# A two-layer HGRN2/mLSTM transformer with experts: router logits from unnormalised rows, expert groups carried across experts, and one order made from simulated times

## The chip, the cores and the metric

The kernel runs on one core of one Trainium2 chip. Its metric is the device time of one execution in microseconds, as a median of runs. The core's engines each work through their own instruction list in order: PE (matmuls and transposes), DVE and ACT (element-wise work), POOL (a few small operations and indirect transfers), and SP, which here issues nearly all DMA transfers.

## The reference, cut to what matters

Two layers on 512 rows of x (and 256 context rows), 1024 wide, all in float32:

```python
for l in range(DEPTH):                         # DEPTH = 2
    mod_x = silu(c) @ w_ada[l] + b_ada[l]      # six vectors of 1024
    hx = x * (1 + mod_x[1]) + mod_x[0]
    mix_x, mix_c = _token_mix(hx, hc, ...)     # w_in, HGRN2 and mLSTM scans, w_out
    x = _layer_norm(ALPHA * x + mod_x[2] * mix_x, ln_g[l, 0], ln_b[l, 0])
    hx = x * (1 + mod_x[4]) + mod_x[3]
    f_x = _channel_mix(hx, l, ...)             # layer 0: dense SwiGLU, layer 1: experts
    x = _layer_norm(ALPHA * x + mod_x[5] * f_x, ln_g[l, 1], ln_b[l, 1])

def _moe_swiglu(h, router_w, router_b, w_gate_up, w_down):      # layer 1
    top_val, top_idx = lax.top_k(h @ router_w + router_b, 2)    # 8 experts
    top_p = softmax(top_val)
    # sum over experts e of combine[:, e] * _swiglu(h, w_gate_up[e], w_down[e])
```

The context rows go through the same steps in layer 0 and end with the mixing of layer 1.

## The kernel before

Every large product is made of three matmuls on operands split into a high and a low part (`wh`, `wl` and `xh`, `xl`, `mm3`, lines 165 to 167), so that weights come by DMA into `wr`, ACT makes `wh` (lines 134, 149) and DVE `wl` (lines 135, 150), 128x1024 elements at a time. In product blocks with 64 rows the two parts of the rows share one matmul, and line 1408 adds the two halves.

The program starts with the conditioning product (`w_ada`, line 275), loads the x and context rows (`xs`, line 932), transposes, scales and splits them, and runs `w_in`. Then come, in layer 0, the two scans, `w_out` and the dense block, and in layer 1 the same scans, `w_out` and the experts.

**Router.** In the last pass of layer 1 over `w_out` each row tile (128 rows; there are four) gets its product (line 979), the residual (`add_x`, line 961), its statistics, and is normalised in place (`finish`, line 893) and stored in `xhd`. `router_tile` then transposes the normalised tile in eight blocks (line 1107), copies them into `xhatT`, and forms the logits (line 1114) with a router matrix `rws` into which scale factors of the conditioning are folded. `router` adds the bias (line 1603) and finds the two best experts; in `moe` ranks are counted by a matmul with ones (lines 1136, 1137), row indices are formed by matmuls with one-hots (line 1213), rows are gathered from `xhd` (line 1245) and transposed (line 1256; `xf` and `xs` are the scaled and split result, lines 1259 to 1263). Beside this, lines 1145 to 1154 scale `xhatT`, transpose it back and store it as residual rows `xd` for the end.

**Experts.** The eight experts are sorted by load into ranks with fixed capacities (256, 192, 128 or 64 rows), in two streams, (0, 1, 2) and (6, 3, 7, 4, 5), whose steps a small planner interleaves by the costs they yield. One expert runs over groups of 256 hidden columns. `first` makes gate and up for a group and `hs` = silu(gate) * up; `turn` transposes `hs` into `hT` (line 1421; lines 1422 and 1423 copy and split it); `second` multiplies by the down weights into accumulators kept for the whole expert. A 256-row expert makes `hT` directly. The order in the code is:

```python
            for f0, nb in groups:
                hT, s = yield from first(f0, nb)
                if prev:
                    yield from second(*prev)
                    yield rates[-1] * prev[2]
                turn(hT, s, nb)
                prev = hT, f0, nb
```

A negative cost in a yield asks the planner to take the same stream next. In the last expert of a stream `ahead` loads what the end needs. After the experts, each row tile gathers its two expert results, adds the residual and is normalised (lines 1565 to 1580).

The instruction lists are made by the framework's scheduler, which orders what the code emits by its own priorities and dependencies; pools of buffers (three `hs`, for instance) limit it.

## Time and profile before

| | |
|---|---|
| time, median of 3 runs (lowest to highest) | 2205.84 us (2203.29 to 2208.99) |
| profiled execution: its time, its span | 2203.97 us, 2201.9 us |
| mean granted clock of PE | 0.968 of full speed |
| busy: PE, PEld, DVE, ACT, POOL | 2065.7, 1748.0, 1463.9, 888.5, 162.4 us |
| DMA | 331.25 MB, mean 150 GB/s |

The span is the stretch that the profiler recorded, from the first instruction to the last. Busy times are sums over each engine's instructions; PE is matmuls, PEld the weight loads beside them. [...] In a timeline or a list of waits, the name behind `<-` in brackets is what ended an engine's idle time. A line number is that of the kernel before.

### The profile page before, as it was taken

The page shows a single profiled execution, that of the slowest core. Times are in us where ns is not written, and L with a number is a line of the kernel's source. Part 1 is how long each engine was busy: PE and PEld are TensorE (multiplying, and loading weights), DVE is VectorE, ACT ScalarE, POOL GpSimd, SP SyncE. Part 2 cuts the span into 40 slices and gives each one's busy share as a digit, 9 for nine tenths or more (in the row PEclk, how much of TensorE's full clock was granted, in tenths as well). Part 3 has the DMA queues.
Part 4 walks back from the last instruction along what each step waited for, and adds up shares of the span by engine and source line. Part 5 has one row for each costly group of instructions (what it writes and reads, how often), then busy time and mean ns, then how long its engine had stood idle before and what let it go on. Part 6 is the DMA issues. An engine that isn't in the chain of part 4 may idle for free. (4 is left out here: it accounts for less than half of the span.)

```text
span 2201.9 us, 31832 instructions
## 1 busy us (share of the span) xinstructions
PE 2065.7 (94%) x12321; PEld 1748.0 (79%) x12321; DVE 1463.9 (66%) x2524; ACT 888.5 (40%) x1409; POOL 162.4 (7%) x163
## 2 busy tenths in 40 slices
PE   8999799999999999999999999999979899798993
PEld 3887688987888888888888788899977787577882
DVE  4466784825787755554555678686678767877776
ACT  3335333323442222211124354334157665766662
POOL 1001000100200000022000000101310000000002
PEclk9999999999999999999999999999869899899996
DMA  7123202146454443322131321124368778888884
GB/s 259 50 69 110 63 27 85 46 142 225 165 183 149 155 138 134 134 77 77 58 106 50 91 68 55 48 63 151 133 210 301 260 265 279 266 271 295 306 280 171
DMA packets 233187, 331.25 MB, mean 150 GB/s; under 512 B 13904, under 2 KB 181012, under 8 KB 233032
## 3 DMA queue, kind: packets, MB, share of 16 engines
q1 hardware_dynamic: 229624, 318.09, 43.5%
q0 software_dynamic: 3408, 11.08, 1.5%
q8 instruction: 99, 1.62, 0.3%
q14 instruction: 56, 0.46, 0.1%
HBM read 304.94 MB, written 24.19 MB: 149 GB/s over the span
## 5 line engine op out<-in xcount | busy, mean ns | idle before, releaser
L165 PE MATMUL g<-xh,wh 128*128 128x512 f32 (+1 forms) x1168 | 400.7, 343 | 1.4 <-ACT xh L380 1.4
L166 PE MATMUL g<-xl,wh 128*128 128x512 f32 (+1 forms) x1168 | 400.3, 343 | 1.5 <-DVE xl L381 1.5
L167 PE MATMUL g<-xh,wl 128*128 128x512 f32 (+1 forms) x1168 | 399.8, 343 | 0.0
L135 DVE TENSOR_TENSOR wl<-wr,wh 128x1024 fp32r<-128x1024 f32 x240 | 293.5, 1233 | 144.0 <-ACT wh L134 142.6
L134 ACT ACTIVATE wh<-wr 128x1024 fp32r<-128x1024 f32 x240 | 249.8, 1056 | 248.7 <-PE sc L167 81.6
L165 PE MATMUL g<-wh,xh 128*128 128x256 f32 x1024 | 296.6, 290 | 9.4 <-ACT wh L134 2.2
L166 PE MATMUL g<-wl,xh 128*128 128x256 f32 x1024 | 296.4, 290 | 2.9 <-DVE wl L131 2.7
L167 PE MATMUL g<-wh,xl 128*128 128x256 f32 x1024 | 294.0, 288 | 0.0
L165 PEld LDWEIGHTS g<-xh,wh 128*128 128x128 f32 x1168 | 220.4, 189 | 30.0 <-issue 1.7
L166 PEld LDWEIGHTS g<-xl,wh 128*128 128x128 f32 x1168 | 220.2, 189 | 27.9 <-DVE xl L381 1.9
L167 PEld LDWEIGHTS g<-xh,wl 128*128 128x128 f32 x1168 | 220.2, 189 | 26.5
L150 DVE TENSOR_TENSOR wl<-wr,wh 128x1024 fp32r<-128x1024 f32 x154 | 185.7, 1219 | 47.6 <-ACT wh L149 46.3
L165 PEld LDWEIGHTS g<-wh,xh 128*128 128x128 f32 x1024 | 196.5, 192 | 15.3 <-ACT slot L766 2.9
L166 PEld LDWEIGHTS g<-wl,xh 128*128 128x128 f32 x1024 | 196.7, 192 | 5.0 <-DVE wl L131 4.4
L167 PEld LDWEIGHTS g<-wh,xl 128*128 128x128 f32 x1024 | 196.4, 192 | 0.0
L149 ACT ACTIVATE wh<-wr 128x1024 fp32r<-128x1024 f32 x154 | 160.4, 1055 | 60.5 <-DMA wr<-in_moe_w_gate_up 43.6
L865 DVE TENSOR_TENSOR s<-g,s 128x512 f32<-128x512 f32 (+1 forms) x44 | 24.4, 555 | 128.4 <-PE g L167 128.4
L463 PE MATMUL sc<-tmp,s 128*128 128x128 f32 x560 | 79.8, 290 | 4.6 <-DVE tmp L471 3.9
L866 ACT ACTIVATE hh<-s 128x512 fp32r<-128x512 f32 (+1 forms) x44 | 23.1, 525 | 144.8 <-DVE s L865 144.8
L463 PEld LDWEIGHTS sc<-tmp,s 128*128 128x128 f32 x560 | 71.6, 193 | 11.2 <-issue 3.9
L520 POOL TENSOR_TENSOR ss<-ss,mhalf 128x4 f32<-128x4 f32 (+1 forms) x22 | 27.3, 1248 | 716.1 <-DVE ss L519 543.5
L458 ACT ACTIVATE s<-slot 128x768 f32<-128x768 f32 (+1 forms) x56 | 44.4, 793 | 78.7 <-DVE slot L469 67.0
(497 smaller groups left out, 4031.9 us busy)
## 6 DMA issues: line engine op xcount, KB each, us to landing
wr<-in_moe_w_gate_up SPq DMA_DIRECT2D x176, 512.0 KB
wr<-in_moe_w_down SPq DMA_DIRECT2D x88, 512.0 KB
wr<-in_w_in SPq DMA_DIRECT2D x64, 512.0 KB
wr<-in_ffn_w_gate_up SPq DMA_DIRECT2D x44, 512.0 KB
wh<-in_w_ada SPq DMA_DIRECT2D x20, 1024.0 KB
wl<-in_w_ada SPq DMA_DIRECT2D x20, 1024.0 KB
wr<-in_ffn_w_down SPq DMA_DIRECT2D x22, 512.0 KB
wr<-in_w_ada SPq DMA_DIRECT2D x16, 512.0 KB
```

The costliest lines, as they stand in the source:

```text
L134: nc.scalar.activation(fl(h), r, AF.Copy)
L135: nc.vector.tensor_tensor(fl(lo), r, fl(h).bitcast(F32), OP.subtract)
L149: nc.scalar.activation(v(h, u), r, AF.Copy)
L150: nc.vector.tensor_tensor(v(lo, u), r, v(h, u).bitcast(F32), OP.subtract)
L165: nc.tensor.matmul(out, ah, bh, start=(i == 0), stop=False)
L166: nc.tensor.matmul(out, ah, bl, start=False, stop=False)
L167: nc.tensor.matmul(out, al, bh, start=False, stop=(i == n - 1))
L458: nc.scalar.activation(apx(kc, 0, [[2 * hh, qn // (2 * hh)], [hh, 2], [1, hh]]), apx(ka, 0, [[2 * hh, qn // (2 * hh)], [hh + T, 2], [1, hh ...
L463: nc.tensor.matmul(pl[:, c - a], kc[:, c * P:(c + 1) * P], apx(qa, c * P + T, [[2 * hh, 64 // hh], [hh - T, 2], [1, hh]]), start=True, sto ...
L520: nc.gpsimd.tensor_tensor(ss[:, :n], ss[:, :n], self.mhalf[:, :n], OP.pow)
L865: nc.vector.tensor_tensor(s, pu, s, OP.mult)
L866: nc.scalar.activation(hh[:, b, t0:t0 + n], s, AF.Copy)
```

## The change

The change has four parts.

1. `TileContext` is opened with `schedule_with_timeline_sim=True`: the scheduler orders all instructions of the program on all engines by a simulated timeline of engines and queues.
2. Router: `router_half` transposes each half of a row tile as soon as the residual is added, before it is normalised, and forms raw logits. In `router`, eight small instructions add minus the mean times the column sums of `rws` (`rsum`, made once by eight matmuls with ones), scale by the reciprocal deviation and add the bias. The normalised rows `xo` go to `xhd` as before.
3. Residual rows are no longer made by transposing `xhatT` back and stored in `xd`; `ahead` loads the rows from `xhd` and two broadcast rows, and eight 1024-wide DVE instructions (`scale`, `shift`) are handed out over the steps of the last big expert.
4. Experts: a group's `turn` and `second` are carried into the next group (`run`), also from one expert into the next of its stream; `turn` is called by `mid` in the middle of the next gate/up product. `rest` finishes the last one. The accumulators are taken when the first `second` begins. `hs` has four buffers. Some small tiles of the planning code share storage (not shown).

```diff
@@ -984,17 +984,20 @@
                     add_x(t, 1)
-                    self.finish(pre[:, t], sts[t], (self.xhd if last else self.xd)[t * P:(t + 1) * P])
+                    if last:
+                        self.router_half(pre, t, 0)
+                        self.router_half(pre, t, 1)
+                        self.router_finish(pre[:, t], sts[t], t, self.xhd[t * P:(t + 1) * P])
+                        continue
+                    self.finish(pre[:, t], sts[t], self.xd[t * P:(t + 1) * P])
                     for u in behind(t, nt):
-                        if last:
-                            self.router_tile(pre, u)
-                        else:
-                            self.split_tile(pre[:, u], u, xh, xl, aff[u // NX], act=u < nt - 2)
+                        self.split_tile(pre[:, u], u, xh, xl, aff[u // NX], act=u < nt - 2)
...
-                self.moe(l, aff[0], pre)
+                self.moe(l, aff[0])
                 break
@@ -1086,34 +1089,44 @@
             nc.sync.dma_start(self.ysd[NSLOT + b * P:NSLOT + (b + 1) * P], zt)
-        self.xt = lp.tile([P, KT, TX], F32, name="xhatT")
+        self.mr = lp.tile([P, NX, 2], F32, name="meanr")
...
-        pb = self.psum("sc", [P, N_E])
-        for k in range(KT):
-            nc.tensor.matmul(pb, self.ones, rt[:, k], start=k == 0, stop=k == KT - 1)
-        nc.vector.tensor_tensor(self.rb, self.rb, pb, OP.add)
+        pb = self.psum("sc", [P, 2, N_E])
+        for i, w in enumerate((rt, self.rws)):
+            for k in range(KT):
+                nc.tensor.matmul(pb[:, i], self.ones, w[:, k], start=k == 0, stop=k == KT - 1)
+        nc.vector.tensor_tensor(self.rb, self.rb, pb[:, 0], OP.add)
+        self.rsum = lp.tile([P, N_E], F32, name="rsum")
+        nc.vector.tensor_copy(self.rsum, pb[:, 1])
         self.plog = self.psum("tr", [P, NX, N_E])
-    def router_tile(self, pre, t):
-        nc = self.nc
-        for hf in range(2):
-            pt = self.psum(("sc", "o")[hf], [P, 4, P])
-            for k in range(4):
-                nc.tensor.transpose(pt[:, k], pre[:, t, (4 * hf + k) * P:(4 * hf + k + 1) * P], self.ident)
-            o = self.xt[:, 4 * hf:4 * hf + 4, t * P:(t + 1) * P]
-            if hf:
-                nc.vector.tensor_copy(o, pt)
-            else:
-                nc.scalar.activation(o, pt, AF.Copy)
-        for k in range(KT):
-            nc.tensor.matmul(self.plog[:, t], self.xt[:, k, t * P:(t + 1) * P], self.rws[:, k], start=(k == 0), stop=(k == KT - 1))
-    def moe(self, l, aff, pre):
+    def router_half(self, pre, t, hf):
+        nc = self.nc
+        pt = self.psum(("sc", "o")[hf], [P, 4, P])
+        for k in range(4):
+            nc.tensor.transpose(pt[:, k], pre[:, t, (4 * hf + k) * P:(4 * hf + k + 1) * P], self.ident)
+        o = self.lp.tile([P, 4, P], F32, tag="preT", name=self.nm("preT"), bufs=4)
+        nc.scalar.activation(o, pt, AF.Copy)
+        for k in range(4):
+            nc.tensor.matmul(self.plog[:, t], o[:, k], self.rws[:, 4 * hf + k], start=hf == 0 and k == 0, stop=hf == 1 and k == 3)
+    def router_finish(self, x, st, t, dst):
+        nc = self.nc
+        mean, r = self.moments(st)
+        nc.vector.tensor_scalar(self.mr[:, t, 0:1], mean, -1.0, None, op0=OP.mult)
+        nc.vector.tensor_copy(self.mr[:, t, 1:2], r)
+        o = self.lp.tile([P, D], F32, tag="xo", name=self.nm("xo"), bufs=2)
+        nc.vector.tensor_scalar(o, x, mean, r, op0=OP.subtract, op1=OP.mult)
+        nc.sync.dma_start(dst, o)
+    def moe(self, l, aff):
@@ -1134,26 +1147,8 @@
         nc.tensor.matmul(pp, self.ones, Mc, start=True, stop=False)
-        mm = nc.tensor.matmul(pp[:, 0:NX], self.trif, M, start=False, stop=True)
-        p0 = tc.cur_priority
-        tc.cur_priority = p0 + 1000
-        gb = self.lp.tile([P, 2, KT], F32, name="gbcol")
-        for i, v in enumerate((self.g_col(l, 0), self.b_col(l, 0))):
-            nc.vector.tensor_scalar(gb[:, i], v, ALPHA, None, op0=OP.mult)
-        for k in range(KT):
-            nc.scalar.activation(self.xt[:, k], self.xt[:, k], AF.Identity, scale=gb[:, 0, k:k + 1], bias=gb[:, 1, k:k + 1])
-        with tc.issue_after(mm.ins):
-            for hf in range(2):
-                for t in range(NX):
-                    pt = self.psum("g", [P, 4, P])
-                    for k in range(4):
-                        nc.tensor.transpose(pt[:, k], self.xt[:, 4 * hf + k, t * P:(t + 1) * P], self.ident)
-                    nc.scalar.activation(pre[:, t, hf * 512:hf * 512 + 512], pt.rearrange("p k c -> p (k c)"), AF.Copy)
-                    if hf:
-                        nc.sync.dma_start(self.xd[t * P:(t + 1) * P], pre[:, t])
+        nc.tensor.matmul(pp[:, 0:NX], self.trif, M, start=False, stop=True)
         self.lp_cm.__exit__(None, None, None)
-        tc.cur_priority = p0
         inc, cnt = small([NX, 8], "inc"), small([8], "cnt")
@@ -1350,23 +1345,22 @@
         def act(pg, pu, shape, parts=P):
-            s = mp.tile([P, 256], F32, tag="hs", name=self.nm("hs"), bufs=3)[:parts, :shape]
+            s = mp.tile([P, 256], F32, tag="hs", name=self.nm("hs"), bufs=HSB)[:parts, :shape]
...
         def expert(n, xs, gu_src, dn_src, acc_tag, write, weight):
...
-            acc = [[self.psum(acc_tag, [P, 512]) for _ in range(2)] for _ in range(nblk)]
-            groups = [(f0, min(256, D_E - f0) // P) for f0 in range(0, D_E, 256)]
-            def first(f0, nb):
+            acc = []
+            def first(f0, nb, mid):
                 fn = nb * P
@@ -1383,6 +1377,8 @@
                         yield 4
+                        if b == 0:
+                            mid()
                     return hT, None
@@ -1395,6 +1391,8 @@
                         st, en = k == 0, k == KT - 1
+                        if i == 0 and k == KT // 2:
+                            mid()
                         if m == P:
@@ -1424,6 +1422,8 @@
                 wd = self.load_w((nb, D), lambda i, j: dn_src(f0 // P + i, j - i))
+                if f0 == 0:
+                    acc.extend([self.psum(acc_tag, [P, 512]) for _ in range(2)] for _ in range(nblk))
                 for m in range(nblk):
@@ -1442,31 +1442,41 @@
-            prev = None
-            for f0, nb in groups:
-                hT, s = yield from first(f0, nb)
-                if prev:
-                    yield from second(*prev)
-                    yield rates[-1] * prev[2]
-                turn(hT, s, nb)
-                prev = hT, f0, nb
-            if prev:
-                yield from second(*prev)
-                yield rates[-1] * prev[2]
-            for m in range(nblk):
-                for half in range(2):
-                    c = slice(512 * half, 512 * half + 512)
...
-        def rank_gen(r, xs, big):
+                yield rates[-1] * nb
+                if f0 + nb * P < D_E:
+                    return
+                for m in range(nblk):
+                    for half in range(2):
+                        c = slice(512 * half, 512 * half + 512)
...
+            return first, turn, second
+        def run(parts, prev):
+            first, turn, second = parts
+            for f0, nb in [(f0, min(256, D_E - f0) // P) for f0 in range(0, D_E, 256)]:
+                hT, ss = yield from first(f0, nb, lambda: [t(h, s, n) for t, _, h, s, _, n in prev])
+                for _, sec, h, _, g, n in prev:
+                    yield from sec(h, g, n)
+                prev[:] = [(turn, second, hT, ss, f0, nb)]
+        def rest(prev):
+            for turn, second, hT, ss, f0, nb in prev:
+                yield -1e-6
+                turn(hT, ss, nb)
+                yield -1e-6
+                yield from second(hT, f0, nb)
+        def rank_parts(r, xs, big):
             e = bass.ds(nc.sync.value_load(expi[0:1, r:r + 1], min_val=0, max_val=7), 1)
@@ -1482,21 +1492,34 @@
                 x = mg.tile([P, NX, D], F32, tag="xsA", name="xrows", bufs=2)
-                nc.sync.dma_start(x, self.xd[0:TX].rearrange("(t p) c -> p t c", p=P))
+                nc.sync.dma_start(x, xhd[:, :].rearrange("(t p) c -> p t c", p=P))
                 xr.extend(x[:, t] for t in range(NX))
-                return
+                ab = []
+                for row in (I["ln_g"][l, 0], I["ln_b"][l, 0]):
+                    g = mg.tile([P, D], F32, tag="gat", name=self.nm("gat"), bufs=3)
+                    nc.sync.dma_start(g, bass.AP(tensor=row.tensor, offset=row.offset, ap=[[0, P], [1, D]]))
+                    ab.append(g)
+                def scale(x):
+                    nc.vector.scalar_tensor_tensor(x, x, ALPHA, ab[0], op0=OP.mult, op1=OP.mult)
+                def shift(x):
+                    nc.vector.scalar_tensor_tensor(x, ab[1], ALPHA, x, op0=OP.mult, op1=OP.add)
+                return [lambda f=f, y=y: f(y) for y in xr for f in (scale, shift)]
...
+            return []
         def stream(ranks, big):
             xs, _ = first[0 if big else 1]
+            prev = []
             for i, r in enumerate(ranks):
                 cur, parts = xs, []
-                for step, c in enumerate(rank_gen(r, cur, big)):
+                for step, c in enumerate(run(rank_parts(r, cur, big), prev)):
                     if step == PREP and i + 1 == len(ranks):
-                        ahead(big)
+                        parts = ahead(big)
                     elif step == PREP:
+            yield from rest(prev)
@@ -1600,7 +1625,9 @@
         lg = fp.tile([P, NX, N_E], F32, name="lg")
-        nc.vector.tensor_tensor(lg, self.plog, self.rb[:, None, :].to_broadcast([P, NX, N_E]), OP.add)
+        for t in range(NX):
+            nc.vector.scalar_tensor_tensor(lg[:, t], self.rsum, self.mr[:, t, 0:1], self.plog[:, t], op0=OP.mult, op1=OP.add)
+            nc.vector.scalar_tensor_tensor(lg[:, t], lg[:, t], self.mr[:, t, 1:2], self.rb, op0=OP.mult, op1=OP.add)
         mx = fp.tile([P, NX, 8], F32, name="mx")
@@ -1629,6 +1656,8 @@
 PREP = 3
+HSB = 4
 STREAMS = ((0, 1, 2), (6, 3, 7, 4, 5))
@@ -1656,7 +1685,7 @@
     out = nc.dram_tensor("out_x", (1, TX, D), F32, kind="ExternalOutput").ap()
-    with tile.TileContext(nc) as tc, ExitStack() as ctx:
+    with tile.TileContext(nc, schedule_with_timeline_sim=True) as tc, ExitStack() as ctx:
         Kern(ctx, tc, aps, out).run()
```

How this moves instructions is read from the instruction lists of both kernels. On PE, behind the last `w_out` matmul (first row), the list before has 24 transposes and 24 logit matmuls:

```order
L167 MATMUL g_13857<-wh_13594,xl_80 128x256
L1107 MATMUL sc_13896<-ident,pre_13256 128x128 x4
L1107 MATMUL o_13902<-ident,pre_13256 128x128 x4
L1107 MATMUL sc_13916<-ident,pre_13256 128x128 x2
L1114 MATMUL tr_13291<-rws,xhatT 128x8 x4
L1107 MATMUL sc_13916<-ident,pre_13256 128x128 x2
L1107 MATMUL o_13922<-ident,pre_13256 128x128 x4
L1114 MATMUL tr_13291<-rws,xhatT 128x8 x12
L1107 MATMUL sc_13936<-ident,pre_13256 128x128 x4
L1107 MATMUL o_13942<-ident,pre_13256 128x128 x4
L1114 MATMUL tr_13291<-rws,xhatT 128x8 x8
```

and now, up to the rank sums (last two rows), this is on PE:

```order
L167 MATMUL g_13922<-wh_13604,xl_80 128x256
L1113 MATMUL sc_13954<-ident,pre_13256 128x128 x4
L1117 MATMUL tr_13301<-rws,preT_13880 128x8 x4
L1117 MATMUL tr_13301<-rws,preT_13959 128x8 x4
L1113 MATMUL o_13965<-ident,pre_13256 128x128 x4
L1117 MATMUL tr_13301<-rws,preT_13970 128x8 x4
L1149 MATMUL tr_14034<-Mc,ones 128x40
L1150 MATMUL tr_14034<-M,trif 128x32
```

`g` is the product, `sc` and `o` the transposes' results, `tr` the logits. Eight transposes and twelve logit matmuls are left behind the last product; the others moved ahead of it.

At a change of experts in the second stream PE has, before, the transposes of gathered rows (`gat`) and of four groups (`hs`) in a row, directly ahead of the down product with `hT`:

```order
L1404 MATMUL g_16935<-wl_16926,xs_15685 128x512
L1256 MATMUL tr_16875<-ident,gat_16642 128x128 x4
L1421 MATMUL g_16971<-ident,hs_16834 128x64 x2
L1421 MATMUL g_17043<-ident,hs_16955 128x64 x2
L1421 MATMUL tr_16909<-ident,hs_16799 128x64 x2
L1421 MATMUL tr_16966<-ident,hs_16720 128x128 x2
L1437 MATMUL g_16370<-wh_17025,hT_16758 128x512
L1438 MATMUL g_16370<-wl_17026,hT_16758 128x512
```

Now the place where the transpose results `g` and `tr` of two groups meet reads as follows on PE, between two down products:

```order
L1438 MATMUL o_16560<-wl_16854,hT_16363 128x512
L1419 MATMUL g_16905<-ident,hs_16797 128x64 x2
L1419 MATMUL tr_16781<-ident,hs_16631 128x64 x2
L1251 MATMUL tr_16800<-ident,gat_16545 128x128 x4
L1437 MATMUL g_16534<-wh_16835,hT_16585 128x512
L1438 MATMUL g_16534<-wl_16836,hT_16585 128x512
```

The transposes of `hs` stand in twos, and the groups whose `hs` they take are not those whose `hT` the next matmuls use.

On SP, at the start, the list before has all loads of `w_ada` (`wr`) ahead of most loads of rows (`xs`):

```order
L273 DMA wr_188<-in_w_ada 128x2x512
L273 DMA wr_192<-in_w_ada 128x2x512
L273 DMA wr_196<-in_w_ada 128x2x512
L273 DMA wr_200<-in_w_ada 128x2x512
L299 DMA adar_204<-in_b_ada 2x512
L932 DMA xs<-in_x 128x1024 x3
L932 DMA xs<-in_ctx 128x1024 x2
L124 DMA wr_427<-in_w_in 128x4x256
```

Now, from the fifth load of `w_ada` on, SP has:

```order
L273 DMA wr_136<-in_w_ada 128x2x512
L273 DMA wr_140<-in_w_ada 128x2x512
L299 DMA adar_152<-in_b_ada 2x512
L932 DMA xs<-in_x 128x1024 x4
L932 DMA xs<-in_ctx 128x1024
L273 DMA wr_144<-in_w_ada 128x2x512
L932 DMA xs<-in_ctx 128x1024
L273 DMA wr_148<-in_w_ada 128x2x512
```

Five of the six row loads moved ahead of ten loads of `w_ada`, the sixth ahead of nine.

## Rows read from the trace of the kernel before

**Rows 1.** By windows, mixing, feed-forward, router and experts; columns in the first line.
```profile
core 0: us, PE busy (x) PEld busy (x) DVE busy (x) ACT busy (x) POOL busy (x), PEclk, DMA share, GB/s
...
50.00:480.00 430.00, 410.86 (x2854) 357.28 (x2853) 272.68 (x562) 157.82 (x268) 32.39 (x28) 0.99 0.24 74
608.00:1170.00 562.00, 561.89 (x2969) 475.31 (x2968) 350.89 (x458) 139.71 (x209) 33.12 (x22) 1.00 0.36 120
1587.30:1621.80 34.50, 27.60 (x162) 25.61 (x160) 20.10 (x100) 16.59 (x26) 3.51 (x4) 0.66 0.36 127
1621.80:1640.00 18.20, 14.16 (x68) 13.28 (x68) 14.94 (x51) 9.77 (x15) 3.31 (x3) 0.51 0.77 264
1640.00:1700.00 60.00, 53.19 (x307) 45.23 (x306) 52.82 (x88) 45.30 (x62) 0.89 (x1) 0.95 0.90 307
1700.00:1760.00 60.00, 52.42 (x292) 44.38 (x292) 43.44 (x57) 36.73 (x55) 2.12 (x2) 0.88 0.74 248
1760.00:1840.00 80.00, 79.89 (x450) 68.80 (x449) 55.21 (x64) 45.21 (x60) 1.54 (x1) 1.00 0.80 264
1840.00:1930.00 90.00, 74.84 (x305) 56.54 (x304) 71.80 (x94) 62.25 (x92) 1.58 (x1) 0.89 0.83 277
1930.00:2040.00 110.00, 101.01 (x463) 79.40 (x463) 82.84 (x103) 71.15 (x97) 0.00 (x0) 1.00 0.84 287
2040.00:2168.00 128.00, 123.77 (x587) 100.34 (x585) 93.47 (x112) 76.32 (x103) 0.00 (x0) 1.00 0.78 266
```

**Rows 2.** Timeline of PE at the router: start, length, engine, line, operation.
```profile
1587.16 0.28 PE L167 MATMUL g<-wh,xl 128*128 128x256 f32 x1
...
1593.71 1.09 PE L1107 MATMUL sc<-ident,pre 128*128 128x128 f32 x4
...
1595.49 3.58 PE L1114 MATMUL tr<-rws,xhatT 128*128 128x8 f32 x16
```

**Rows 3.** Timeline of DVE there; in brackets the idle time before, and its releaser.
```profile
1587.48 0.42 DVE L979 TENSOR_TENSOR pre<-g,bc 128x256 f32<-128x256 f32 x1 [2.42 <-PE g L167]
1587.94 0.69 DVE L961 TENSOR_TENSOR pre<-pre,xr 128x512 f32<-128x512 f32 x1
...
1592.10 0.81 DVE L893 TENSOR_SCALAR pre<-pre,mv,r 128x1024 f32<-128x1024 f32 x1 [0.73 <-POOL r L842]
...
1599.11 0.19 DVE L1603 TENSOR_TENSOR lg<-tr,rb 128x32 f32<-128x32 f32 x1 [2.72 <-PE tr L1114]
```

**Rows 4.** Timelines of SP and PE just ahead of the first expert.
```profile
1610.03 0.41 SPq L124 DMA_DIRECT2D wr<-in_moe_w_gate_up  x1
1611.72 3.26 SPq L1154 DMA_DIRECT2D xd<-pre  x4
1623.68 1.57 SPq L124 DMA_DIRECT2D wr<-in_moe_w_gate_up  x3
...
1616.72 0.90 PE L1256 MATMUL o<-ident,gat 128*128 128x128 f32 x3 [1.97 <-DMA gat<-xhd,ix]
```

**Rows 5.** Waits of PE, 1621 to 2168 us (sum, times, longest): three of 26.
```profile
PE g L1421 <- DVE hT L1423: 3.9, 2, 2.0
PE tr L1256 <- ACT xf L1259: 3.6, 2, 2.7
...
PE sc L1441 <- ACT hT L1422: 0.2, 1, 0.2
```

**Rows 6.** Timelines of DVE and PE at one change of experts.
```profile
1923.10 1.21 DVE L135 TENSOR_TENSOR wl<-wr,wh 128x1024 fp32r<-128x1024 f32 x1
...
1925.17 0.69 PE L1421 MATMUL tr<-ident,hs 128*128 128x128 f32 x2 [2.07 <-DVE hT L1423]
```

**Rows 7.** By windows, the end of the start; columns as in rows 1.
```profile
40.00:50.00 10.00, 5.89 (x39) 4.78 (x40) 9.62 (x19) 9.97 (x22) 0.00 (x0) 0.95 0.35 96
```

**Rows 8.** Timeline of DVE for the last tile of the output.
```profile
2193.22 1.23 DVE L1571 SCALAR_TENSOR_TENSOR row<-row,row 128x1024 f32<-128x1024 f32 x1
...
2196.00 0.15 DVE L1574 TENSOR_SCALAR fr<-fsq 128x1 f32<-128x1 f32 x1 [1.36 <-ACT row L1573]
```

More of the change, by code (lines that the diff above doesn't have):

```diff
@@ L1557, in write @@
                 nc.sync.dma_start(ysv[bass.ds(iv, 1), :, c].rearrange("b p c -> (b p) c"), y)
-            for _ in expert(P, xs, gs, ds_, "accB", write, lambda m: ow):
+            prev = []
+            for _ in itertools.chain(run(expert(P, xs, gs, ds_, "accB", write, lambda m: ow), prev), rest(prev)):
                 pass
```

34 lines of the change are left out of this document (17 added, 17 removed).

## The prediction

> **What bounds the kernel now.** I read the table by windows first, since one share for the whole run (PE 94%) mixes stages with different limits. In the feed-forward block of layer 0 PE is busy 561.89 of 562 us at full clock [rows 1]: no reordering can win there. The first mixing block loses 19.1 us of 430 [rows 1]. What is lost densely lies behind 1587 us. The router stretch lasts 34.5 us at a granted clock of 0.66. Then come the experts, from 1621.8 us to the last matmul a little before 2168: their seven stretches have 4.0 + 6.8 + 7.6 + 0.1 + 15.2 + 9.0 + 4.2 = 46.9 us without PE work (the last one reaches some us past the last matmul), and lower clocks cost busy time as well, 14.16 x 0.49 + 53.19 x 0.05 + 52.42 x 0.12 + 74.84 x 0.11 = 24 us. So about 70 of 546 us are there to be won, and 11 of them in the first 18 us. The stretch 1760 to 1840 shows what the same code does undisturbed: 79.89 of 80 us at 1.00.
>
> Second, the waits of PE in that stage [rows 5]. The 26 rows sum to 42.9 us. Grouped by what was late: hT, the transposed hidden tile of an expert, 11.8 us; xf and xs, the next expert's gathered rows, 8.2; L1408 of the 64-row blocks 5.1; hs 2.1; the index one-hots 2.9; split weights 12.8. No one engine explains these. DVE is busy 414 of the 546 us (the sum of its column [rows 1]), but it works in order. At a change of experts, a weight split of 1.21 us begins at 1923.10 with the small hT instruction behind it, and PE stands 2.07 us at the next transpose until hT is done [rows 6].
>
> Third, the timelines around the router. The last w_out matmul starts at 1587.16; transposes of the normalised rows still start at 1593.71 and logit matmuls at 1595.49, the latter for 3.58 us [rows 2]; DVE has the logits only at 1599.11 [rows 3]. SP issues the first expert weight load at 1610.03, then the four xd writes, then the next three loads at 1623.68, 13.65 us behind the first [rows 4].
>
> **The change part by part.** The sum is made against the profiled execution's own 2203.97 us; the median of the runs shown is 2205.84, so 1.9 us are added at the end.
>
> *Router.* Transposes and logits now need only the unnormalised row half. Behind the last w_out matmul remain L979 and L961, which end at 1588.63 [rows 3], four transposes (1.1, a group of four in [rows 2]), a copy of 512 columns (0.7, by L961), and four logit matmuls (half of 3.58, whose 16 records are eight matmuls of the program: 1.8): 1592.2. Beside it run the moments: from the end of L961 to L893 they took 3.5 us before, with two tile copies on DVE in between that are now ACT's, so they give r between 1590.7 and 1592.1. By the order of DVE, two small copies and the 1024-wide xo (0.81, as L893) stand ahead of the logits, then eight small instructions of 0.1 to 0.19. The logits end at 1593 to 1595 instead of 1599.3: 4.5 to 6.5 us, I take 5.5. The 32 transposes, their copies and the four xd writes go; PE then stood 1.97 us for gathers that shared the queues with those writes [rows 4], I count 2. Together **-7.5** (bounds -4 to -11: only the short end of the chain, or also everything that stood between rank and gather).
>
> *Weight stream at the start of the experts.* Without the xd writes the second load can follow when the earlier buffers are free, not behind writes that wait for ACT. That stretch loses 11 us [rows 1]; the first expert's second weight half comes from the load at 1623.68. The new PE order also puts index matmuls between expert matmuls. I take **-5**, near half (bounds 0, if the second load waits for the gathers as long, to -9).
>
> *Experts pipelined.* The transposes of a group now stand in the middle of the next group's gate/up matmuls, with half a group as cover for hs, and the down matmuls behind all of it, across experts too. hT and hs (13.9 us) should no longer end PE's waits; of the L1408 waits I count half (2.5); that is 16.4 of 42.9. The clock lost behind 1640 is 17 us; in proportion 6.5 come back. Of the 8.2 us of xf and xs I count 2, since the switch hint goes that held a stream at its boundary. Sum **-25**. Bounds: -5, if the waits turn into waits for split weights, to -45, if of 43 + 17 us only the weight waits stay. hT gets no more cover than half a group: eight to twelve matmuls.
>
> *Residual rows.* Eight new 1024-wide instructions at 1.23 us, by L1571 [rows 8], are 9.8 us of DVE, spread over the last big expert's steps. DVE has 34.5 us free in 2040 to 2168 [rows 1], which covers them; in order they delay a split now and then: **+1** (0 to +5; all 9.8 if DVE had no gap there). Two broadcast loads replace the writes.
>
> *Start.* The six row loads now stand behind the sixth w_ada load on SP (one of them behind the seventh). From 40 to 50 us PE is busy 5.89 of 10 while ACT has 9.97 and DVE 9.62 [rows 7]: PE waits for the splitting of x tiles, which can now begin earlier. Against it, 2.6 MB more ahead of ten w_ada loads take 8.5 us at 307 GB/s [rows 1]. **-2** (-6 to +5).
>
> *Order of the rest.* Mixing blocks: **-1** (-10 to +10; 19 us are lost in the first one, and a new order can halve that or add as much). Feed-forward: 0, PE has no gap; cover is not needed. Tail: the last tile's final work moves ahead of another tile's, which fills the 1.36 us for which DVE waited [rows 8]: **-1** (0 to -1.4).
>
> Sum: -7.5 - 5 - 25 + 1 - 2 - 1 - 1 = -40.5, so 2163.5 in this execution's terms and **2165 us** as a median.
>
> **Rules that bear on it.** While weights flow, the best stretch has 307 GB/s, with a DMA share of 0.90 [rows 1]. Over the seven stretches 150 MB move (rate times length), which at 307 GB/s take 488 us: the stream allows 58 us of gain, not 25 only. [...]
>
> The router stretch is full of transposes and short matmuls and runs at 0.66, although PE is busy 27.6 of 34.5 us [rows 1]. The change takes transposes out there and puts others between expert matmuls. [...] In the boundary [rows 6] idle time and transposes come together, and the trace does not separate them.
>
> **The rivals.** *The stream or the splits set the pace (18 in 100).* PE is held at expert boundaries by waits on wh and wl instead. For it: 12.8 of 42.9 us are already that, and in 1640 to 1700 DVE is busy 88% and DMA 0.90. Against it: the stream has room for 58 us, and 1760 to 1840 runs at 264 GB/s without a gap. The experts then give 5 instead of 25: 2185 us.
>
> *Slower: the new order blocks PE in the mixing blocks (13 in 100).* The whole program is reordered by modelled times; PE works in order, so one matmul put ahead of late DVE or ACT data stops all behind it. There, idle time is 19.1 in 430 us; the mixing stages are about 975 us (50 to 608 and 1170 to 1587), some 43 us at that share. If the new order loses twice that, +43, the gain is eaten; the point where it decides is 40 us. At +50: 2215 us. Against it: filler matmuls between the small steps stay of the same kind.
>
> *Deeper gain (9 in 100).* All but the weight waits go and the clock stays at 1.00: experts -45, so 2145 us; with better mixing 2130.
>
> *The pipelining changes nothing (3 in 100)*, as the order before was already free to move these transposes: experts 0, 2190 us.
>
> **How the numbers follow.** My forecast has 57 in 100, with a range of its own of 2150 to 2180 us. The 80% range reaches to the deep gain below and to the break-even above: 2130 to 2206 us. A measurement of this kernel tells about 0.3%, 6.6 us, from no change. Faster than 2199: nearly all of the forecast, the stream rival, the deep gain and the last one, less what their unknown costs take back, 0.80. Within 0.3%: 0.07, from the edges of the stream and the slower rival. Slower: 0.13.
>
> **What would show it.** Right: the first MAX8 on DVE 4.5 to 6.5 us nearer to the last w_out matmul; no gap of 13 us between the first two expert weight loads; the hT rows nearly gone from PE's waits, and PE over 97% busy at 1.00 in 1840 to 2040. Wrong: hT waits as large as before, weight waits over 25 us, more than 40 us of PE idle added ahead of 1587, or a w_ada stage that ends over 5 us later with nothing gained behind it.

## The result, and the profile after

The changed kernel is slower: 2410.9 us (median of 4 runs, 2407.19 to 2412.86) against 2204.89 us for the kernel before on the same chip, a ratio of 1.0936 (95% interval 1.0912 to 1.096), or +206 us. The profiled execution took 2407.19 us, 203 more than that of before. The page of after, with the busy times and the granted clock of PE in 40 slices (PEclk, the share of full speed that PE was granted, here in tenths):

```profile
PE 2111.8 (88%) x12305; PEld 1788.3 (74%) x12305; DVE 1478.7 (61%) x2542; ACT 880.3 (37%) x1396; POOL 159.5 (7%) x163
...
PEclk9998699998999999999999989986969899798996
```

Before, PE was busy 2065.7 of 2201.9 us (a mean clock of 0.968; now 0.928). So of the 203 us, 157 are idle time of PE (293 instead of 136), and 46 are longer busy time: nearly the same matmuls (12305 records instead of 12321) at a lower clock.

Where the time came is read from a few marks of the program that both traces have: the first key transposes of the mLSTM (L671), the first HGRN level (L450), the first and last feed-forward matmul, the last w_out product, the first expert matmul, the last matmul.

| stretch (us) | before | after | difference |
|---|---|---|---|
| start to first key transposes, layer 0 | 130.5 | 133.5 | +3 |
| mLSTM chunks, layer 0 | 122.7 | 154.7 | +32 |
| HGRN, gates and w_out, layer 0 | 348.2 | 374.1 | +26 |
| feed-forward, to its last down matmul | 572.3 | 590.5 | +18 |
| layer 1 up to its key transposes | 81.4 | 82.4 | +1 |
| mLSTM chunks, layer 1 | 90.6 | 126.6 | +36 |
| HGRN, gates and w_out, layer 1 | 241.5 | 275.8 | +34 |
| router, last w_out product to first expert matmul | 34.7 | 36.3 | +2 |
| experts | 542.6 | 593.7 | +51 |
| tail | 37.4 | 37.5 | 0 |

Nearly every stage pays. The windows of after are the chunks of layer 0, their second part, the feed-forward block, and the chunks and the rest of the mixing in layer 1; the last line sums windows over the experts, cut at the same marks as the seven of [rows 1]:

```profile
core 0: us, PE busy (x) PEld busy (x) DVE busy (x) ACT busy (x) POOL busy (x), PEclk, DMA share, GB/s
133.50:288.20 154.70, 113.41 (x730) 93.54 (x729) 79.94 (x195) 57.95 (x97) 13.19 (x12) 0.84 0.22 70
235.00:288.00 53.00, 22.44 (x112) 18.82 (x112) 26.35 (x65) 12.32 (x23) 6.42 (x6) 0.60 0.06 20
662.30:1252.80 590.50, 577.83 (x3027) 485.63 (x3028) 361.81 (x481) 143.05 (x217) 32.01 (x24) 0.99 0.35 118
1335.20:1461.90 126.70, 114.47 (x782) 99.66 (x780) 68.61 (x161) 48.36 (x86) 8.77 (x8) 0.93 0.24 72
1461.90:1737.70 275.80, 225.48 (x1559) 211.62 (x1560) 176.83 (x307) 80.92 (x147) 37.98 (x42) 0.88 0.22 73
...
sum 594.00, PE 519.15 PEld 422.14 DVE 415.36 ACT 343.15 POOL 10.91; mean PE 74.16 PEld 60.31 DVE 59.34 ACT 49.02 POOL 1.56
```

The same stretches before (chunks of layer 0, feed-forward, chunks and rest of the mixing in layer 1):

```profile
130.50:253.20 122.70, 110.19 (x742) 88.55 (x740) 80.56 (x196) 58.05 (x97) 14.15 (x12) 0.99 0.28 89
601.40:1173.70 572.30, 570.70 (x3008) 482.10 (x3009) 359.91 (x477) 144.93 (x220) 34.22 (x24) 1.00 0.36 122
1255.10:1345.70 90.60, 89.41 (x636) 76.45 (x634) 66.10 (x161) 49.17 (x81) 8.40 (x8) 1.00 0.28 79
1345.70:1587.20 241.50, 232.11 (x1700) 217.83 (x1700) 176.84 (x309) 81.26 (x151) 39.54 (x43) 0.97 0.29 94
```

In layer 1 the table alone misleads: 146 more matmuls lie in the chunk stretch of after and 141 fewer behind it, so much of the +36 is work that moved. PE's idle time there grows by 11 us in the chunk stretch and by 41 behind it. In layer 0 it grows by 29 and by 21. So 62 of the 102 us of idle time that the mixing blocks add lie behind the chunks. Among the experts PE idles 75 us instead of 47 [rows 1], and its busy time grows by 20.

In layer 0 the matmuls of the chunk stretch are nearly the same (730 and 742), but in after they crowd into the first part, and from 235 us on PE is busy 22 of 53 us at a granted clock of 0.60. The waits of PE over the whole run (sum, times, longest) name the places:

```profile
PE o L728 <- issue: 42.3, 4, 11.1
PE o L370 <- DVE tmp L816: 23.0, 2, 12.0
PE sc L450 <- DVE s L795: 19.2, 4, 7.5
PE sc L463 <- DVE tmp L471: 14.5, 9, 2.7
PE g L165 <- ACT wh L134: 10.5, 9, 1.9
PE tr L1251 <- DVE hT L1421: 9.0, 4, 3.1
```

The first is a wait that the profile cannot put down to a semaphore ("issue"). The timelines of PE and DVE in one chunk show what it is:

```profile
241.01 2.09 PE L728 MATMUL o<-early,tmp 128*128 128x129 f32 x8
...
255.35 1.20 PE L728 MATMUL o<-early,tmp 128*128 128x129 f32 x4 [11.10 <-issue]
...
244.98 0.17 DVE L739 SCALAR_TENSOR_TENSOR den<-num 128x8 f32<-128x8 f32 x1 [8.54 <-ACT num L736]
...
249.27 1.54 DVE L702 TENSOR_TENSOR s<-mp,tmp 64x256 f32<-64x256 f32 x4
250.85 2.85 DVE L709 SCALAR_TENSOR_TENSOR tmp<-tmp,u,mneg 128x128 f32<-128x128 f32 x8
...
254.82 1.42 DVE L719 TENSOR_TENSOR tmp<-sc,tmp 128x256 f32<-128x256 f32 x4 [0.52 <-ACT tmp L710]
```

and in before:

```profile
192.36 1.16 PE L728 MATMUL o<-early,tmp 128*128 128x129 f32 x8
...
194.90 0.17 DVE L739 SCALAR_TENSOR_TENSOR den<-num 128x8 f32<-128x8 f32 x1 [5.26 <-ACT num L736]
...
204.73 1.42 DVE L719 TENSOR_TENSOR tmp<-sc,tmp 128x256 f32<-128x256 f32 x4 [0.53 <-ACT tmp L710]
```

One mLSTM chunk is a chain PE, ACT, DVE, ACT, DVE, PE. DVE finishes the old chunk (L739 to L519) and then prepares the next one (L702, L709, L719) while PE stands 11.1 us. DVE's order is the same before, and takes as long (194.90 to 206.15 us). What before has in these 11 us is products of w_in (L165 to L167), 10.2 us per chunk in most of them. By counting their rows (0.119 us for each matmul of 256 columns, 0.231 for 512): from chunk to chunk, before has 16.2, 12.1, 10.2, 10.2, 5.7 (and 7.5 us of w_ada) and 10.2 us of them; after has 28.5, 19.0, 15.6 (and 7.5), 0.7, 0 and 0. They are spent too early. The price has a second part: the eight L728 matmuls that took 1.16 us at 192.36 us in before take 2.09 us at 241.01 us in after. The granted clock is 1.00 from 192.3 to 206.2 us in before, and 0.50 from 241.0 to 243.1 us in after.

### The profile page after: what moved, and what is told of

Same layout as the page of the kernel before. It is cut to its first block, busy times and chain, and to the rows that moved or that the text cites. A ratio compares the mean times of both kernels' runs of the same rounds, so it can differ in the third digit from the quotient of the medians.

```text
span 2405.1 us, 31882 instructions
## 1 busy us (share of the span) xinstructions
PE 2111.8 (88%) x12305; PEld 1788.3 (74%) x12305; DVE 1478.7 (61%) x2542; ACT 880.3 (37%) x1396; POOL 159.5 (7%) x163
## 5 line engine op out<-in xcount | busy, mean ns | idle before, releaser
L165 PE MATMUL g<-xh,wh 128*128 128x512 f32 (+1 forms) x1168 | 403.9, 346 | 22.7 <-ACT wh L134 10.5
L167 PE MATMUL g<-xh,wl 128*128 128x512 f32 (+1 forms) x1168 | 400.0, 344 | 0.0
L134 ACT ACTIVATE wh<-wr 128x1024 fp32r<-128x1024 f32 x240 | 246.3, 1054 | 217.8 <-DMA wr<-in_ffn_w_gate_up 37.5
L165 PE MATMUL g<-wh,xh 128*128 128x256 f32 x1024 | 299.4, 293 | 11.1 <-ACT slot L807 4.9
L167 PE MATMUL g<-wh,xl 128*128 128x256 f32 x1024 | 293.6, 288 | 0.0
L165 PEld LDWEIGHTS g<-xh,wh 128*128 128x128 f32 x1168 | 222.0, 190 | 56.0 <-ACT wh L134 14.4
L167 PEld LDWEIGHTS g<-xh,wl 128*128 128x128 f32 x1168 | 221.9, 190 | 27.4 <-issue 0.3
L165 PEld LDWEIGHTS g<-wh,xh 128*128 128x128 f32 x1024 | 197.8, 194 | 16.9 <-ACT slot L807 6.1
L167 PEld LDWEIGHTS g<-wh,xl 128*128 128x128 f32 x1024 | 197.3, 193 | 0.1
L149 ACT ACTIVATE wh<-wr 128x1024 fp32r<-128x1024 f32 x154 | 158.8, 1055 | 93.4 <-DMA wr<-in_moe_w_gate_up 47.6
L463 PE MATMUL sc<-tmp,s 128*128 128x128 f32 x560 | 86.7, 307 | 18.4 <-DVE tmp L471 14.5
L463 PEld LDWEIGHTS sc<-tmp,s 128*128 128x128 f32 x560 | 79.3, 211 | 23.8 <-issue 12.0
L466 DVE COPY_PREDICATED s<-lmask,sc 128x512 f32<-128x512 uint8 x84 | 50.9, 638 | 62.9 <-PE sc L463 62.7
L864 ACT ACTIVATE s<-g 128x512 f32<-128x512 f32 (+1 forms) x44 | 21.4, 486 | 162.6 <-PE g L167 146.7
```

Of the source, the lines that this page charges most:

```text
L134: nc.scalar.activation(fl(h), r, AF.Copy)
L149: nc.scalar.activation(v(h, u), r, AF.Copy)
L165: nc.tensor.matmul(out, ah, bh, start=(i == 0), stop=False)
L167: nc.tensor.matmul(out, al, bh, start=False, stop=(i == n - 1))
L463: nc.tensor.matmul(pl[:, c - a], kc[:, c * P:(c + 1) * P], apx(qa, c * P + T, [[2 * hh, 64 // hh], [hh - T, 2], [1, hh]]), start=True, sto ...
L466: nc.vector.copy_predicated(AT[:, a:b], self.lmask[:, lev:lev + 1, :].to_broadcast([P, b - a, P]), pl)
```

## The experiments

### Which edit costs the time

**All edits, default order.** The changed kernel with `tile.TileContext(nc)` again; nothing else differs.

> All edits of the change, but the program ordered by the scheduler's default instead of the simulated timeline. Theory A (the order by the simulated timeline costs everything, in the mixing blocks and among the experts, and the edits themselves gain): faster than before, 2160 to 2195 us; the three waits of 11 us at L728 and the two of 11 to 12 us at L370 are gone. Theory B (the edits cost the time: groups carried across experts need buffers and accumulators that aren't free): 2350 us or more, PE stalls between 1780 and 2370 as in the changed kernel. Theory C (mixing blocks lose by the order, the experts by the edits): about 2250 us, experts still about 590 us long.

Measured: 2206.74 us, ratio 1.0006 (0.9987 to 1.0026). Theory A is right on the order and wrong on the edits, which were to gain: together they cost nothing and give nothing. The order is the whole loss.

**The order alone.** One line on the kernel before:

```diff
-    with tile.TileContext(nc) as tc, ExitStack() as ctx:
+    with tile.TileContext(nc, schedule_with_timeline_sim=True) as tc, ExitStack() as ctx:
```

> The kernel before, with the simulated timeline for the order and no other edit. Theory A: slower by 180 to 260 us, 2385 to 2465 us, with waits of 11 us at L728 in the first mixing block. Theory B: within 1% of before. Theory C: about 2350 us, the lost time all ahead of the experts, these 540 us long as before.

Measured: 2408.22 us, ratio 1.0912 (1.0884 to 1.094). That the order is the cause holds from both sides. The experts as they were before take 599.0 us in this order instead of 542.6, so their loss does not come from the pipelining either.

### Why the order costs it

**Products tied behind chunks.** On the order alone, each w_in product of the first HGRN pair may not be issued ahead of a given chunk's last matmul:

```diff
+    def pin(self, cost):
+        k = sum(self.cum >= x for x in self.pin_at)
+        self.cum += cost
+        return self.tc.issue_after(self.pins[k - 1]) if self.pin_on and k else nullcontext()
...
-                p = self.gemm_T(wv_, xh, xl, t, 256)
+                with self.pin(2.9):
+                    p = self.gemm_T(wv_, xh, xl, t, 256)
...
+PIN = ((15, 27, 37, 47, 53, 63), (15, 27, 38, 51))
```

> The kernel before with the simulated order (2408 us alone), and one more edit: the independent w_in products that fill PE beside the mLSTM chunks are tied behind the last matmul of one chunk each (some 8 to 14 us of them for every chunk; issue order only, no wait for data). Theory A1 (the simulated order spends this filler ahead of the early chunks, and the late chunks then leave PE idle for 11 us each): the waits of 11 us at L728 shrink to 3 us or less, the first mixing block is 25 to 35 us shorter, the whole 2365 to 2385 us. Rival A2 (the chunks' own chain on DVE and ACT is ordered badly, whatever PE fills with): chunks still 19 to 20 us apart, the whole within 10 us of 2408.

Measured: 2396.36 us, ratio 1.0874 (1.0838 to 1.0909): 12 us back by the medians and 8 by the ratios, nearer to A2. The long L728 waits of layer 0 shrank from 11.1 to between 2.5 and 7.0 us, but the chunks still took 16 to 25 us. The timeline of ACT shows what I had put in their way:

```profile
178.39 1.28 ACT L703 ACT_TABLE_LOAD   x1
179.68 0.63 ACT L703 ACTIVATE s<-s 128x512 f32<-128x512 f32 x1
180.33 1.28 ACT L785 ACT_TABLE_LOAD   x1
181.63 0.38 ACT L785 ACTIVATE slot<-g 128x256 f32<-128x256 f32 x1
...
182.30 1.28 ACT L710 ACT_TABLE_LOAD   x1
183.60 1.06 ACT L710 ACTIVATE tmp<-tmp 128x1024 f32<-128x1024 f32 x1
```

The evacuations of the tied products (sigmoids, L785) fall between the two exponentials of the chunk (L703, L710), and in these rows a table load of 1.28 us stands on the chain ahead of each of the three. L785 has 13 of them in this kernel; the same instruction has 7 in the order alone (L775). So this run could not settle the question, and the next one asks it from the other side.

**The products first, in the old order.** On the kernel before, the chunks of layer 0 get a later place, so that all w_in products stand ahead of them; nothing else moves.

```diff
+        self.tc.cur_priority += LATE[l]
         for c in (range(NX) if last else ORDER[0]):
...
+        self.tc.cur_priority -= LATE[l]
...
+LATE = (1000, 0)
```

> The kernel before, ordered as before, with one thing moved: the six mLSTM chunks of layer 0 stand behind all the w_in products (64 us of matmuls) that before lie between them. In the changed kernel the first chunks have 28.5, 19 and 15.6 us of these products beside them and the last three none, and there a chunk takes 19.8 us at a granted clock of 0.60. Theory A (the cost of the mixing block is that the products are used up before the chunks, which then run as a bare chain at half clock): six chunks of about 19.8 us follow about 70 us of products, so that the stretch of the chunks and their products grows from 124 us to about 185: +45 to +70, 2250 to 2275, with the granted clock near 0.6 over the chunks. Rival B (where the products stand does not matter, it is the chain's own order): within 12 us of before, 2195 to 2215.

Measured: 2267.85 us, ratio 1.0282 (1.0263 to 1.03). The stretch of the chunks grew from 122.7 to 186.3 us (128.4 to 314.7), nearly the whole loss; no other stage changed by more than 3.4 us. Its windows:

```profile
130.00:200.00 70.00, 69.96 (x458) 56.85 (x458) 24.01 (x53) 24.15 (x44) 0.00 (x0) 1.00 0.32 99
...
220.00:320.00 100.00, 42.85 (x209) 37.99 (x210) 55.79 (x134) 21.53 (x40) 13.70 (x12) 0.54 0.09 32
```

Seventy microseconds of products without a gap, and then a bare chain at 0.54. PE stands about 11 us ahead of each of five chunks, and they cost 63.6 us, some 12.7 each: theory A. The changed kernel has three such chunks in layer 0, which would be 38 us at that price; its stretch grew by 32.

**One stage in the new order.** The kernel before, with only the mixing of layer 0 ordered by the simulated timeline:

```diff
-            self.mix(l, xh, xl, last)
+            with nullcontext() if last else tc.block(schedule_with_timeline_sim=True):
+                self.mix(l, xh, xl, last)
```

> The kernel before, with only the mixing of layer 0 ordered by the simulated timeline; all the rest in the default order. Theory A (the +60 us of this stage come from the order within it): +45 to +70, 2250 to 2275, the last chunks at 19.8 us as in the changed kernel. Rival B (the cost comes from how the stage is ordered against the one before and the one behind): below +20, 2205 to 2225.

Measured: 2290.56 us, ratio 1.0381 (1.0362 to 1.04), +84 us by the ratio, which is more than A said. The chunks took 154.6 us (148.4 to 303.0), as in after, the last of them 19.8 us apart, and the rest up to the feed-forward block 381 us (after 374). The other 18 us lie ahead of the chunks, which start at 148.4 instead of 130.5: presumably work of this stage that had been drawn in beside the one before and now begins at the block's edge. So A is right on the cause, and the edge is a cost of the experiment. PE's waits here:

```profile
PE o L728 <- issue: 33.9, 4, 11.1
PE sc L450 <- DVE s L795: 12.4, 2, 7.5
PE o L370 <- DVE tmp L816: 11.9, 1, 11.9
PE g L165 <- ACT wh L130: 10.9, 1, 10.9
```

The first three are rows of after too. The fourth stands at the stage's other end, where `w_out` begins (592 us): its weights were not split ahead of that, which is probably the edge again.

**The experts as a block, default order, and the same block in the new order.** On all edits without the whole-program order:

```diff
-                self.moe(l, aff[0])
+                with tc.block():
+                    self.moe(l, aff[0])
```

and `tc.block(schedule_with_timeline_sim=True)` in the second kernel.

> All edits in the default order, with the expert stage (from rank sums to the end) traced into a block of its own that is scheduled as a unit. It is the control for the next kernel: nothing of the stage may be ordered among what is ahead of it. I expect 2207 to 2225 us (prefetches that no longer cross the border).

> As the control, but the block of the expert stage alone is ordered by the simulated timeline. Theory A (the order costs the experts some 50 us by itself, without what the mixing blocks lose): 40 to 60 us slower than the control, with hT and hs again in PE's waits. Rival (the experts of the changed kernel are slow because they begin in another state, with weights not yet loaded): within 10 us of the control.

Measured: 2206.5 us, ratio 1.0017 (0.9998 to 1.0035), and 2260.91 us, ratio 1.0263 (1.0229 to 1.0298). The order of the expert stage alone costs 54 us, as much as after loses there (51). The control came out half a us below its range, and the second kernel at theory A. PE's waits in the second:

```profile
PE tr L1252 <- DVE hT L1422: 8.3, 3, 3.1
PE g L1420 <- DVE hs L1351: 7.1, 2, 3.8
PE g L1442 <- ACT hT L1421: 6.9, 6, 1.7
```

The pipelined generators only offer work; in the new order PE comes to transposes and down products before `hs` and `hT` are ready, and waits for them, up to 3.8 us at a time in these rows. PE's idle time among the experts is 78 us against 37 in the control, and its busy time 15 us longer. Why the simulated times place them so was not tested.

### What the edits are worth in the old order

**Router and residual rows alone.** The kernel before with `router_half`, `router_finish` and the residual rows, the old experts, default order.

> The kernel before with the router's and the residual rows' part alone (default order, experts as before, three hs buffers). My terms: logits 6 us earlier, gathers 2 us, weight stream at the start 5 us, DVE +1: 2190 to 2198 us. Rival (these chains were hidden or are given back by waits for weights): 2200 to 2210 us.

Measured: 2199.38 us, ratio 0.9976 (0.996 to 0.9991), between the two ranges.

**The same with the transposes two tiles behind again:**

```diff
-                        self.router_half(pre, t, 0)
-                        self.router_half(pre, t, 1)
                         self.router_finish(pre[:, t], sts[t], t, self.xhd[t * P:(t + 1) * P])
+                        for u in behind(t, nt):
+                            self.router_half(pre, u, 0)
+                            self.router_half(pre, u, 1)
```

> The router part alone in the default order, as before, but the transposes and logit matmuls of a tile stand two tiles behind its products again. Theory A (moved ahead of the last products on a busy TensorE they took back what the shorter chain gave): the last w_out product ends 5 to 8 us earlier, the router's stretch stays at 30 to 32 us, and the time is 4 to 8 us below the router part's 2199.4: 2191 to 2195. Rival B (the last matmuls now stand behind the last product again, and the stretch grows back to 34): 2197 to 2202.

Measured: 2197.44 us, ratio 0.9974 (0.9956 to 0.9992): B. PE in the first and then in the second of the two kernels, from the last product on:

```profile
1597.06 0.29 PE L167 MATMUL g<-wh,xl 128*128 128x256 f32 x1
...
1600.82 1.87 PE L1117 MATMUL tr<-rws,preT 128*128 128x8 f32 x8 [0.75 <-ACT preT L1115]
1606.49 0.65 PE L1149 MATMUL tr<-Mc,ones 128*128 128x40 f32 x2 [3.79 <-DVE Mc L1147]
```

```profile
1590.22 0.28 PE L167 MATMUL g<-wh,xl 128*128 128x256 f32 x1
...
1598.15 3.42 PE L1118 MATMUL tr<-rws,preT 128*128 128x8 f32 x16
1605.37 0.65 PE L1150 MATMUL tr<-Mc,ones 128*128 128x40 f32 x2 [3.79 <-DVE Mc L1148]
...
1609.88 0.99 PE L1209 MATMUL sc<-tid,oh 128*128 128x2 f32 x4 [3.45 <-DVE oh L1204]
```

From the last product to the counts (`Mc`) it takes 9.4 us in the first and 15.2 in the second, but the last product comes 7 us later in the first. The transposes and logit matmuls are PE's own work; they stand either ahead of the last products or behind them. Before, the counts started at 1602.09, earlier than in both; measured from the first HGRN level of layer 1, they start after 256.4 us before, 257.9 in the first and 258.2 in the second. The one-hot products also slowed down: four took 0.71 us at 1611.97 in before, among the transposes that this edit removes, and take 0.99 in the row above. The granted clock was 0.70 from 1602.0 to 1613.5 us in before, and is 0.50 from 1605 to 1612 us in the second kernel. What the edit did give lies behind: the experts took 537.6 and 535.4 us instead of 542.6.

**The pipelined experts alone**, old router, default order.

> The kernel before with the pipelined experts alone (default order, router and residual rows as before). My term: 25 us less, 2175 to 2185 us, with hT gone from PE's waits. Rival (stalls turn into waits for split weights, or the default order had already overlapped the groups): 2195 to 2210 us. Theory B: over 2230 us.

Measured: 2201.4 us, ratio 0.9973 (0.9955 to 0.9992), in the rival's range, and, in the profiled execution, an expert stage of 542.6 us, the same as before. PE's waits in it, to be held against [rows 5]:

```profile
PE g L1442 <- ACT wh L134: 5.1, 3, 2.1
PE g L1406 <- ACT wh L149: 4.6, 5, 1.6
PE g L1407 <- DVE wl L150: 3.4, 3, 1.4
PE g L1443 <- DVE wl L135: 2.8, 3, 1.6
```

The hT rows are gone (11.8 us before, under 1 now), and the waits for split weights have grown from 12.8 to some 22 us.

**A quarter of the low splits on POOL**, on all edits in the default order, to see whether the splits set the pace (`lo_eng` gives POOL for every fourth split from the experts on, and else DVE):

```diff
-            nc.vector.tensor_tensor(fl(lo), r, fl(h).bitcast(F32), OP.subtract)
+            self.lo_eng().tensor_tensor(fl(lo), r, fl(h).bitcast(F32), OP.subtract)
```

> All edits in the default order (2207 us), with every fourth low-part split of expert weights on POOL instead of DVE (66 of 264, at about 2.1 us each by the 512-wide POOL row of 1.08 us, against 1.23 us on DVE). Theory D (after the pipelining PE's waits are for weight splits that queue on DVE in order): weight waits fall and the time with them, 2185 to 2200 us. Rival (a split on POOL comes late itself, or the wait is for ACT and the transfer): 2203 us or more.

Measured: 2237.27 us, ratio 1.015 (1.0121 to 1.0178). By groups of instructions, POOL and DVE in this kernel, and DVE's same split without it:

```profile
L156 POOL TENSOR_TENSOR wl<-wr,wh 128x1024 fp32r<-128x1024 f32 x36 | 94.1, 2613 | 203.2 <-ACT wh L155 164.6 <-DVE wl L156 14.9 <-PE g L1405 12.8
...
L156 DVE TENSOR_TENSOR wl<-wr,wh 128x1024 fp32r<-128x1024 f32 x118 | 160.3, 1372 | 77.4 <-ACT wh L155 76.6
```

```profile
L150 DVE TENSOR_TENSOR wl<-wr,wh 128x1024 fp32r<-128x1024 f32 x154 | 186.1, 1219 | 54.9 <-ACT wh L149 53.7
```

The time fits the rival. POOL takes 2.61 us for a split of 1.22, and DVE's own take 1.37 us in this run. The run leaves open why DVE's splits take longer in it, and whether splits at full speed on another engine would help.

**All edits, default order, transposes two tiles behind:**

> All of the change except the order from a simulated timeline, with the router's transposes two tiles behind again. Theory A (each part is worth what it gave alone, and the weight stream sets the pace of the experts): 4 to 8 us below the 2206.7 of all the edits, 2198 to 2203, and no better than the router part alone. Rival B (the pipelined experts hide the weights once the router is earlier): 2185 to 2195.

Measured: 2203.91 us, ratio 0.9998 (0.998 to 1.0015), outside both ranges and nearer to A. Each part alone is a quarter of a per cent faster than before (ratios 0.9976 and 0.9974 for the router, 0.9973 for the experts); together they give nothing. These gains are at the limit of what the runs can tell, and no run shows why they do not add.

## Why the prediction was wrong

**Order of the rest, mixing blocks: -1 (-10 to +10).** This step failed. The two mixing blocks lost 132 us (3 + 32 + 26 in layer 0; 1 + 36 + 34 in layer 1). The rival that it was weighed against, a new order that blocks PE in the mixing blocks, named the mechanism and a break-even of 40 us, but it priced it by the wrong row: the 43 us that PE idles there now, once more (+43 to +50). Ahead of the last w_out product PE's idle time grew by 113 us (48.5 to 161.8), where the prediction's own sign of being wrong was 40.

The idle time of the old order says how well that order covers its chains, not what the chains take bare. The bare price could have been read in the trace of before: DVE takes 11.25 us from one chunk's L739 to the end of the next one's L719, with 10.2 us of products beside it on PE. The argument against the rival, that filler stays of the same kind, was true and beside the point: there was as much filler in layer 0 (64.7 and 63.7 us in the chunk stretch), at another place. That the order does it is shown by the order alone and by the single stage, and the price of a bare chunk by the products put first. Not taken apart by a run of its own is the part behind the chunks, with 62 of the 102 us of idle time, whose waits are the L450, L463 and L370 rows. In layer 1 the same cause is likely there: counted as above, the chunk stretch has 82.0 us of products instead of 61.1, and the stretch behind it 127.6 instead of 153.8.

**Feed-forward: 0, since PE has no gap.** It lost 18 us. In before PE waits there for no split weights; in the new order it waits nine times for `wh`, 10.5 us, and over the whole stage it is busy 577.8 of 590.5 us instead of 570.7 of 572.3. A stage without gaps has nothing to win, and it can still lose.

**Experts pipelined: -25.** In the default order the stage is as long as before, and the time 2.6 us less by the medians: hT's waits went, as the step said, and weight waits took their place; the step's own lower bound named this, at -5, and still kept too much for the stage. This speaks for the rival that the stream or the splits set the pace, but no run shows which of the two. In the new order +51. The forecast that hT rows would be nearly gone held only without that order: in after hT ends 27 us of PE's waits among the experts, 11.8 before.

**Router: -7.5.** The chain was sized rightly. From L979 to the end of the logits after takes 5.7 us, before 11.8 [rows 3]; the step said 4.5 to 6.5 less. These are the rows of DVE in after:

```profile
1738.02 0.42 DVE L979 TENSOR_TENSOR pre<-g,bc 128x256 f32<-128x256 f32 x1 [3.17 <-PE g L167]
...
1743.10 0.63 DVE L1630 SCALAR_TENSOR_TENSOR lg<-lg,meanr,rb 128x8 f32<-128x8 f32 x4
```

What failed is the assumption that the moved transposes and logit matmuls cost nothing ahead of the last product. PE has no room there, so the last product came as much later. In the new order even the stretch behind it is not shorter: 36.3 us, where the same edits in the default order take 29.8. The router's granted clock, with fewer transposes, is 0.58 over these 29.8 us; it was 0.66 over the 34.5 us of [rows 1]. No run shows the 2 us that the step counted for the gathers: without the xd writes PE stands 2.42 us for them in the first router kernel and 2.63 us in the second, where it stood 1.97 [rows 4]. Nor did the two share a queue: from 1607 to 1623 us the trace of before has 1.31 MB on q0, the size of the 320 gathered rows, and 2.62 MB on q1, that of the four writes and a weight load.

**Weight stream: -5.** Right in the default order. SP now issues the first four expert loads together:

```profile
1754.54 2.68 SPq L124 DMA_DIRECT2D wr<-in_moe_w_gate_up  x4
```

and the 13.65 us gap of [rows 4] is gone; in the two router kernels in the default order the experts became 5.0 and 7.2 us shorter, with the residual rows' +1 in the same number. The 307 GB/s that the prediction took for the best rate is that of its own stretches: from 31.6 to 40.0 us the trace of before moves 378 GB/s, so the stream had more room than it reckoned.

**Start -2, residual rows +1, tail -1.** The w_ada matmuls of the start end at 41.6 instead of 37.3 us, and a little of that is won back by the first key transposes (+3, inside its bounds). The tail did not gain (37.4 and 37.5 us). The residual rows have no run of their own.

The chances failed with the first step: 13 in 100 for the side that came, and a range that ended at its break-even.

## What to carry to other kernels

A change of the rule that orders a whole program is not bounded by the idle time that it could win. Ask of each stage what its chain takes bare, how much filler lies beside it, and what happens when the filler comes first; a stage without gaps has nothing to win and can still lose. Then work that is moved from behind an engine's last instruction to ahead of it gains only if that engine has gaps there. And a wait that is removed is worth something only if the next-latest input (here split weights) is early.

## What the runs showed of the hardware

A bare chain costs twice here: in idle time (up to 11.1 us at a time ahead of L728 in after), and by its own matmuls at a lower granted clock. It was 0.60 from 235 to 288 us in after and 0.54 from 220 to 320 us with the products put first, against 0.99 over the whole chunk stretch of before; eight L728 matmuls took 2.09 instead of 1.16 us.

With the residual transposes among them, four one-hot products of the router took 0.71 us, and without them (the second router kernel) 0.99. The granted clock was 0.70 from 1602.0 to 1613.5 us in the first case and 0.50 from 1605 to 1612 us in the second. PE's idle time differs too (it was busy 10.2 of the 11.5 us in the first case, and stood 3.45 us just ahead of these products in the second), and no run separates it from the transposes.

A table load of 1.28 us falls on the chunk's chain when sigmoid evacuations are put between its exponentials. In the timeline of ACT above, 178.39 + 1.28 = 179.67 and the next instruction starts at 179.68; that one ends at 180.31 and the next load starts at 180.33. So in these rows 0.01 us lies between a load and the instruction behind it, and 0.02 us between that one and the next load.
